# A two-layer attention trunk on one core: one tiling for the small matrix products, and the second layer's scale and shift computed inside the first layer's value products

## The chip, the cores and the metric

The kernel runs on one core of one Trainium2 chip, as one launch. The metric is device time in microseconds (us), from the start of the launch to its end. Before the change the median of three runs is 308.79 us (307.97 to 309.48).

A core has a matrix engine (TensorE; PE in the profile, with its weight loads listed apart as PEld), three engines that work on vectors (VectorE or DVE, ScalarE or ACT, GpSimd or POOL) and an engine that issues transfers (SyncE or SP). Each engine takes its own instructions strictly in the order in which they were written. SBUF is the on-chip memory, PSUM the memory that the matrix engine writes into.

## What is computed

The input is 256 tokens of width 1024. Two layers follow, each of this form:

```python
for i in range(DEPTH):                      # 2 layers
    shift, scale, gate = jnp.split(cond @ ada_w[i] + ada_b[i], 3, axis=-1)
    h = rms_norm(x, norm_g[i]) * (1 + scale[:, None, :]) + shift[:, None, :]
    y = nsa_mixer(h, ...) if i == 0 else moba_mixer(h, ...)
    x = x + gate[:, None, :] * y
```

`cond` is one row of 1024 numbers, `ada_w[i]` is 1024 x 3072. So scale and shift of a layer come from a product of one row with 2048 columns, and the gate from one with 1024 columns.

The first mixer is causal attention with 16 query heads and 4 key/value heads of width 64, in three branches whose results are added with a learned weight each: a windowed branch, a selected branch (with 256 tokens, all blocks are selected, so that it is causal attention with keys and values of its own), and a compressed branch. For the compressed branch, 15 overlapping blocks of 32 tokens are turned by a small two-layer network into one key and one value each. All is multiplied by `silu(z)` and goes through an output matrix:

```python
hid   = gelu(flat @ cmp_w1[i] + cmp_b1[i])          # blocks of 32 tokens x 64 -> 256
o     = g0 * softmax(q k_cmp) v_cmp + g1 * softmax(q k_sel) v_sel + g2 * softmax(q k_win) v_win
y     = (o * silu(z)) @ w_out
```

The second mixer is plain causal attention of the same shape with one branch. Everything is float32.

## The kernel before

**Precision.** The large products are made of three faster ones. A weight block of 128 x 1024 (`raw`) is rounded by ScalarE into `hi`, VectorE computes the rest `lo`, and the matrix engine adds hi x hi, hi x lo and lo x hi. Products whose operands stay plain float32 run as two matmul instructions each, so the profile counts two where the code has one call.

**Stages, in order of time.** The first 66 us or so load, scale and project the first layer's keys and values. Then come the compressing network (`cmp_steps`), the queries (`make_q`), the compressed keys and values, the gate blocks z (`z_blocks`), the first layer's attention (`pair_a(i)` for eight pairs of heads, i = 0 to 7), the output product (`out_products`), `next_h` for the second layer, its projections, its attention (`pair_b`, `values_b`) and its output product.

**Tiled products.** The matrix engine is an array of 128 x 128. A product that needs only some of its columns or rows can be placed on a part of it (`tile_position`), and several such parts work at the same time. The kernel before uses three ways of cutting:

- 128 rows x 32 columns, four parts: scale and shift (`ada_rows`, `ada_all`). The weights are the conditioning row in a 128 x 32 block (`condz`), and the data are 128 x 512 pieces of `ada_w`.
- 128 rows x 64 columns, two parts: the values (`values`, for both layers) and the compressing network (`cmp_steps`). For values, the two parts are the two heads of a pair.
- 32 rows x 128 columns, four parts: the compressed values. `Vbd` holds, for each pair j of a half (hf), 32 rows: 16 compressed blocks for each of two heads, in a block-diagonal form. `pcT` holds the transposed probabilities of eight heads in its 128 rows, so pair j needs rows 32j to 32j + 31. For two pairs at a time, this product opens the accumulators `ov[hf, j]`, to which `values` then adds.

**Side work.** `side` is a list of generators that run one step at a time where the program calls `beside()`: the four steps of the compressing network, then `ada_all` (the second layer's scale and shift, eight steps of two 512 KB loads and four products each, and an end with a copy, four transposes and three small VectorE operations into `AB`), then `ada_gate(0)` (a memset, eight steps of one 512 KB load and one VectorE accumulation into `gate`, and an end with two products and two copies). `beside()` is called once per step of the query product (four times), once for three of the z steps, and three times in each pair of the first six.

**Who decides the order.** The program does not run as it is written. `Plan` records every operation with what it reads and writes, and `issue` then orders the operations of each engine with a cost model: at each step the earliest possible operation of all engines is issued, ties being settled by level (FIRST_OF_ALL, URGENT, CHAIN, FILL) and then by number. A `plan.group()` is one unit that stays together. For the matrix engine the model adds `SWITCH` when the way of cutting changes, prefers tiled work while it is in a tiled state (`TILED`), and halves the clock after a stretch of 3.4 us with little work. `LATER_BY` moves single operations up or down among their equals by number, and `HOLD` gives single operations an earliest time. `Tag`s are sets of buffers: `raw` has 6, `ps` (PSUM) 6, `n_out` 2. SyncE issues all large loads in the planned order and waits where a buffer isn't free.

All instructions are written through one recording helper, so they all carry its line, L406, in the profile. They are told apart by the names of what they write and read: `ps<-raw,condz` is scale and shift of the second layer, `ps<-pT,VA` the values, `ps<-pcT,Vbd` the compressed values, `ps<-p,p` and `ps<-zT,p` the compressing network, `gate<-raw,condz,gate` the accumulation of a gate.

Of the kernel before, what the change touches and what calls it, by code (L numbers as in the profile page):

```python
# [56 lines left out]
    120: 16500, 167: 22100, 305: 52600, 312: 37600, 383: 32300, 385: 34800, 390: 48600, 395: 51100, 499: 79600,  # L57
    503: 79600, 951: 114700, 1239: 173400, 1371: 179400, 1543: 193600, 1558: 197000, 1625: 208400, 1715: 225000,
    1717: 227500, 1746: 205600, 2238: 273000,
# [13 lines left out]
class Plan:  # L73
# [179 lines left out]
    def issue(self, opening=()):  # L253
# [51 lines left out]
        while done < len(ops):  # L305
# [58 lines left out]
            if e == "T":  # L364
                tick = int(start // TICK)
                if op["mode"] != mode:
                    cost += SWITCH
                mode = op["mode"]
                cost = cost * (1 / 2.4 if tally.get(tick - 1, 0.0) >= 3060.0 else 1 / 1.2)
                tally[tick] = tally.get(tick, 0.0) + op["cost"]  # L370
                if (start + cost) // TICK > tick:
                    cost += PAUSE
# [61 lines left out]
def kernel(  # L434
# [133 lines left out]
    emask = const.tile([P, 2], F32, name="emask")  # L568
    V.tensor_reduce(emask, identF.rearrange("p (j e n) -> p e j n", e=2, n=16), axis=AX.XY, op=OP.add)
# [157 lines left out]
    def ada_all():  # L727

        acc = tile_of("ps", 512)
        for kk in range(8):  # L730
            w = [ada_piece(1, kk, c0, D)[:, 0] for c0 in (0, D)]
            with plan.at(FILL), plan.group():
                for s in range(2):
                    for h in range(2):
                        j = 2 * s + h
                        T.matmul(acc[32 * j:32 * j + 32], condz[:, kk], w[s][:, 512 * h:512 * h + 512],
                                 start=(kk == 0), stop=(kk == 7), tile_position=(0, 32 * j))
            if kk < 7:
                yield
# [214 lines left out]
    def values(o, parts, first):  # L954

        with nullcontext() if plan.open else plan.group():
            for n, (v, pT) in enumerate(parts):
                for e in range(2):
                    T.matmul(o[64 * e:64 * e + 64, 0:S], v[0], pT[e][:, 0:S], start=(first and n == 0), stop=False,
                             tile_position=(0, 64 * e))  # L960
                for e in range(2):
                    T.matmul(o[64 * e:64 * e + 64, P:S], v[1], pT[e][:, S:S + P], start=False,
                             stop=(n == len(parts) - 1), tile_position=(0, 64 * e))
# [248 lines left out]
    def cmp_steps(hid):  # L1212

        for kq in range(4):
            w1 = [[load(bass.AP(tensor=nsa_cmp_w1.tensor, offset=nsa_cmp_w1.offset + (kv * 2048 + kq * 512 + k * P) * 256,
                                ap=[[256, P], [P * 256, 2], [1, 256]]), W1_HOME[k // 2]) for kv in range(2)] for k in (0, 2)]
            with plan.at(FILL), plan.group():
                for k in range(4):
                    for kv in range(2):
                        T.matmul(hid[64 * kv:64 * kv + 64, 0:256],  # L1220
                                 FLAT[kv][kq // 2][:, 4 * (kq % 2) + k].rearrange("p g n -> p (g n)"), w1[k // 2][kv][:, k % 2, :],
                                 start=(kq == 0 and k == 0), stop=(kq == 3 and k == 3), tile_position=(0, 64 * kv))
# [4 lines left out]
    side += [cmp_steps(hid), ada_all(), ada_gate(0)]  # L1227
# [65 lines left out]
    Vbd = const.tile([P, 2, P], F32, name="Vbd")  # L1293
    for hf in range(2):
        for cc in range(2):
# [5 lines left out]
        V.tensor_mul(Vbd[:, hf].rearrange("p (e d) -> p e d", e=2),  # L1301
                     vb[:, None, hf * HD:(hf + 1) * HD].to_broadcast([P, 2, HD]),
                     emask[:, :, None].to_broadcast([P, 2, HD]))
# [10 lines left out]
    pcT, ov = {}, {}  # L1314

    def compressed(hf):
# [25 lines left out]
        A.copy(pcT[hf], t[:, 0:S])  # L1342

    def pair_a(i):
# [36 lines left out]
        if j_ % 2 == 0:  # L1381
            with plan.group():
                for j in range(j_, j_ + 2):
                    ov[hf, j] = tile_of("ps", 512)
                    T.matmul(ov[hf, j][:, 0:S], Vbd[32 * j:32 * j + 32, hf], pcT[hf][32 * j:32 * j + 32],
# [182 lines left out]
```

## Time and profile before

| | before |
|---|---|
| median of three runs | 308.79 us (307.97 to 309.48) |
| span of the profiled execution | 306.3 us |
| PE busy | 297.5 us, 97% of the span |
| VectorE busy | 248.7 us, 81% |
| ScalarE busy | 203.0 us, 66% |
| read from device memory | 64.36 MB |
| granted clock of the matrix engine, mean | 0.998 |

The page gives the span of the profiled execution, from its first to its last instruction, and no time of its own for that execution; the median lies 2.5 us above the span. Busy times of the matrix engine include the pipeline of each instruction, so that its work is better read from the distance of the starts of successive instructions. "Waited for" in the profile means the idle time just before an instruction and what ended it; "issue" is idle time that nothing in the profile explains.

### The profile page before, as it was taken

The numbers are of one execution on the slowest core, as the hardware profiler recorded it, in microseconds if no ns is written. First come the engines' busy times: TensorE is split into PE (matmuls) and PEld (weight loads), VectorE is DVE, ScalarE is ACT, GpSimd is POOL, SyncE is SP. The second block draws the span as 40 slices with busy tenths as digits, with TensorE's granted clock in tenths as the row PEclk, the third lists the DMA queues.
The fourth block names the chain that finished last, engine by engine and source line by source line (L and its number), as shares of the span: only waits on it lengthen the run. The fifth ranks groups of instructions, "written<-read, shape, count | busy, mean of one in ns | idle before, by whom it ended". The sixth has DMA issues, their size and how long they took to land.

```text
span 306.3 us, 6115 instructions
## 1 busy us (share of the span) xinstructions
PE 297.5 (97%) x2097; PEld 242.2 (79%) x2097; DVE 248.7 (81%) x736; ACT 203.0 (66%) x484; POOL 29.4 (10%) x100
## 2 busy tenths in 40 slices
PE   4999999999999999999999999999999999999995
PEld 4666777868878696878897788787788999878784
DVE  3674474678799988799999897797599999999664
ACT  4735244674937795679877985766566589999510
POOL 8128980000000000000000000000000000000000
PEclk9999999999999999999999999999999999999999
DMA  8999999699974294968558269036477780441002
GB/s 250 321 355 368 367 355 342 229 271 323 347 284 149 63 372 140 346 207 328 162 185 274 70 205 329 17 76 224 131 258 235 235 285 4 149 131 67 2 34 103
DMA packets 41099, 65.80 MB, mean 215 GB/s; under 512 B 4220, under 2 KB 20970, under 8 KB 41068
## 3 DMA queue, kind: packets, MB, share of 16 engines
q1 hardware_dynamic: 40708, 65.36, 65.0%
q8 instruction: 16, 0.26, 0.3%
q14 instruction: 15, 0.12, 0.1%
q10 hardware_dynamic: 168, 0.06, 0.1%
q0 software_dynamic: 192, 0.00, 0.0%
HBM read 64.36 MB, written 1.05 MB: 214 GB/s over the span
## 4 chain that ended last, share of the span: by engine, by line
PE 82%; DVE 6%; ACT 5%; DMA 4%; issue 2%; ACTq 0%; SPq 0%; DVEq 0%
PE ps L406 46%; PE acc L406 36%; DVE p L406 3%; ACT p L406 2%; DMA y<-in_ada_b_dram 2%; DMA early<-in_nsa_w_in_dram 1%; DMA raw<-in_nsa_w_out_dram 1%; DVE lo L406 1%; ACT pT L406 1%; ACT n_out L406 1%; DVE tiny L406 0%; ACT hi L406 0%; ACT HT L406 0%; ACT qg L406 0%; ACTq L406 0%
## 5 line engine op out<-in xcount | busy, mean ns | idle before, releaser
L406 ACT CAST hi<-raw 128x1024 fp32r<-128x1024 f32 (+1 forms) x48 | 49.2, 1027 | 17.1 <-PE acc L406 14.8
L406 DVE TENSOR_TENSOR lo<-raw,hi 128x1024 fp32r<-128x1024 f32 (+1 forms) x48 | 56.7, 1188 | 3.1 <-ACT hi L406 2.8
L406 ACT ACTIVATE p<-p,tiny 128x128 f32<-128x128 f32 (+1 forms) x96 | 43.2, 459 | 10.7 <-DVE tiny L406 10.6
L406 PE MATMUL acc<-hi,HT 128*128 128x512 f32 (+1 forms) x160 | 49.6, 383 | 0.0
L406 PE MATMUL acc<-HT,hi 128*128 128x256 f32 x192 | 39.1, 288 | 0.0
L406 PEld LDWEIGHTS acc<-hi,HT 128*128 128x128 f32 x160 | 28.8, 188 | 6.7 <-issue 1.2
L406 DVE CUSTOM_DVE_ANT_0 p<-ps,causal 128x128 f32<-128x128 f32 (+1 forms) x96 | 31.3, 356 | 1.5 <-PE ps L406 1.5
L406 PEld LDWEIGHTS acc<-HT,hi 128*128 128x128 f32 x192 | 30.5, 189 | 0.9 <-issue 0.7
L406 PE MATMUL acc<-lo,HT 128*128 128x512 f32 (+1 forms) x80 | 30.4, 384 | 0.4 <-DVE lo L406 0.4
L406 PE MATMUL ps<-hi,HT 128*128 128x512 f32 (+1 forms) x96 | 29.0, 367 | 0.0
L406 PE MATMUL ps<-KTA,qg 128*128 128x256 f32 (+2 forms) x192 | 27.3, 282 | 0.0
L406 PE MATMUL acc<-HT,lo 128*128 128x256 f32 x96 | 27.3, 286 | 0.0
L406 PEld LDWEIGHTS ps<-KTA,qg 128*128 128x128 f32 x192 | 24.2, 189 | 3.3 <-issue 1.2
L406 PE MATMUL ps<-hi,qg 128*128 128x256 f32 (+1 forms) x96 | 24.4, 324 | 0.0
L406 PE MATMUL acc<-hi,qg 128*128 128x512 f32 x64 | 23.3, 415 | 0.0
L406 ACT COPY pT<-ps 128x384 f32<-128x384 f32 x48 | 21.1, 492 | 2.3 <-PE ps L406 2.3
L406 DVE TENSOR_TENSOR lo<-early,hi 128x1024 fp32r<-128x1024 f32 (+2 forms) x17 | 17.4, 1041 | 5.4 <-ACT hi L406 5.0
L406 ACT CAST hi<-early 128x1024 fp32r<-128x1024 f32 (+2 forms) x17 | 14.8, 897 | 10.3 <-DMA early<-in_nsa_w_in_dram 8.5
L406 PE MATMUL ps<-identF,p 128*128 128x128 f32 x144 | 21.0, 275 | 0.2
L406 PEld LDWEIGHTS ps<-hi,HT 128*128 128x128 f32 x96 | 17.2, 188 | 4.6 <-issue 1.9
L406 DVE SCALAR_TENSOR_TENSOR gate<-raw,condz,gate 128x1024 f32<-128x1024 f32 x16 | 20.5, 1283 | 0.0
L406 PEld LDWEIGHTS ps<-identF,p 128*128 128x128 f32 x144 | 16.2, 140 | 3.8 <-DVE p L406 0.9
(218 smaller groups left out, 618.8 us busy)
## 6 DMA issues: line engine op xcount, KB each, us to landing
raw<-in_ada_w_dram SPq DMA_DIRECT2D x32, 512.0 KB, 5.7
raw<-in_moba_w_in_dram SPq DMA_DIRECT2D x20, 512.0 KB, 4.7
early<-in_ada_w_dram SPq DMA_DIRECT2D x12, 512.0 KB, 9.6
raw<-in_nsa_w_in_dram SPq DMA_DIRECT2D x12, 512.0 KB, 6.6
early<-in_nsa_w_in_dram SPq DMA_DIRECT2D x9, 512.0 KB, 9.2
raw<-in_nsa_w_out_dram SPq DMA_DIRECT2D x8, 512.0 KB, 4.6
raw<-in_moba_w_out_dram SPq DMA_DIRECT2D x8, 512.0 KB, 4.0
early<-in_nsa_w_in_dram SPq DMA_DIRECT2D x9, 256.0 KB, 6.0
```

The source lines that it names most:

```text
L406: r = getattr(self.engines[e], method)(*[self._real(a) for a in args], **{k: self._real(a) for k, a in kw.items()})
```

## The change

It has five parts.

1. **One tiling.** `values` and `cmp_steps` cut the array into four parts of 128 x 32 in place of two of 128 x 64: each call becomes two, with half of the weight columns each.
2. **Zero-padded compressed values.** `Vbd` becomes 128 x 2 x 4 x 128: for each pair it holds all 128 rows, with zeros outside the pair's 32 rows and outside the block diagonal. `emask` gets eight columns for it. The product takes all of `pcT`, in four parts of 128 x 32, and stands at the head of the pair's own values group. The accumulator is taken there, one for each pair. `Vbd` lives in a buffer of `n_out` now.
3. **Scale and shift of the second layer in the values groups.** `ada_all` leaves `side` and becomes `along`. Its first loads are recorded ahead of the first pair; step i's four products join the values group of pair i, and the loads of the next step follow. Its end comes with pair 7.
4. **Side work.** With `ada_all` gone, the gate's steps come sooner (the first in the fourth step of the query product, three in z), and each pair has one step.
5. **Plan.** The model keeps the full clock for every operation that starts after 20 us (`DEEP`), and `LATER_BY` and `HOLD` are another table, for the new numbers.

```diff
 LATER_BY = [
-    (109, 110, -64), (255, 255, 155), (307, 310, -51), (316, 317, -56), (330, 330, 298), (350, 350, 26),
...
+    (96, 96, 56), (161, 161, -76), (308, 308, -51), (309, 309, -14), (330, 330, 286), (345, 345, 357),
...
 HOLD = {
-    120: 16500, 167: 22100, 305: 52600, 312: 37600, 383: 32300, 385: 34800, 390: 48600, 395: 51100, 499: 79600,
...
+    93: 15600, 167: 22100, 235: 24800, 387: 44100, 390: 47900, 522: 63700, 781: 109200, 930: 121400, 1080: 117700,
...
-                cost = cost * (1 / 2.4 if tally.get(tick - 1, 0.0) >= 3060.0 else 1 / 1.2)
+                cost = cost * (1 / 2.4 if start > DEEP or tally.get(tick - 1, 0.0) >= 3060.0 else 1 / 1.2)
...
-    emask = const.tile([P, 2], F32, name="emask")
-    V.tensor_reduce(emask, identF.rearrange("p (j e n) -> p e j n", e=2, n=16), axis=AX.XY, op=OP.add)
+    emask = const.tile([P, 8], F32, name="emask")
+    V.tensor_reduce(emask, identF.rearrange("p (h n) -> p h n", n=16), axis=AX.X, op=OP.add)
...
             w = [ada_piece(1, kk, c0, D)[:, 0] for c0 in (0, D)]
-            with plan.at(FILL), plan.group():
-                for s in range(2):
-                    for h in range(2):
-                        j = 2 * s + h
-                        T.matmul(acc[32 * j:32 * j + 32], condz[:, kk], w[s][:, 512 * h:512 * h + 512],
-                                 start=(kk == 0), stop=(kk == 7), tile_position=(0, 32 * j))
-            if kk < 7:
-                yield
+            yield
+            for s in range(2):
+                for h in range(2):
+                    j = 2 * s + h
+                    T.matmul(acc[32 * j:32 * j + 32], condz[:, kk], w[s][:, 512 * h:512 * h + 512],
+                             start=(kk == 0), stop=(kk == 7), tile_position=(0, 32 * j))
+            yield
...
             for n, (v, pT) in enumerate(parts):
-                for e in range(2):
-                    T.matmul(o[64 * e:64 * e + 64, 0:S], v[0], pT[e][:, 0:S], start=(first and n == 0), stop=False,
-                             tile_position=(0, 64 * e))
-                for e in range(2):
-                    T.matmul(o[64 * e:64 * e + 64, P:S], v[1], pT[e][:, S:S + P], start=False,
-                             stop=(n == len(parts) - 1), tile_position=(0, 64 * e))
+                for j in range(4):
+                    T.matmul(o[32 * j:32 * j + 32, 0:S], v[0][:, j % 2 * 32:j % 2 * 32 + 32], pT[j // 2][:, 0:S],
+                             start=(first and n == 0), stop=False, tile_position=(0, 32 * j))
+                for j in range(4):
+                    T.matmul(o[32 * j:32 * j + 32, P:S], v[1][:, j % 2 * 32:j % 2 * 32 + 32], pT[j // 2][:, S:S + P],
+                             start=False, stop=(n == len(parts) - 1), tile_position=(0, 32 * j))
...
-                    for kv in range(2):
-                        T.matmul(hid[64 * kv:64 * kv + 64, 0:256],
-                                 FLAT[kv][kq // 2][:, 4 * (kq % 2) + k].rearrange("p g n -> p (g n)"), w1[k // 2][kv][:, k % 2, :],
-                                 start=(kq == 0 and k == 0), stop=(kq == 3 and k == 3), tile_position=(0, 64 * kv))
+                    for j in range(4):
+                        kv, half = divmod(j, 2)
+                        flat = FLAT[kv][kq // 2][:, 4 * (kq % 2) + k].rearrange("p g n -> p (g n)")
+                        T.matmul(hid[32 * j:32 * j + 32, 0:256], flat[:, 32 * half:32 * half + 32], w1[k // 2][kv][:, k % 2, :],
+                                 start=(kq == 0 and k == 0), stop=(kq == 3 and k == 3), tile_position=(0, 32 * j))
...
-    side += [cmp_steps(hid), ada_all(), ada_gate(0)]
+    side += [cmp_steps(hid), ada_gate(0)]
+    along = ada_all()
...
-    Vbd = const.tile([P, 2, P], F32, name="Vbd")
+    Vbd = tile_of("n_out", 2, 4, P)
...
-        V.tensor_mul(Vbd[:, hf].rearrange("p (e d) -> p e d", e=2),
-                     vb[:, None, hf * HD:(hf + 1) * HD].to_broadcast([P, 2, HD]),
-                     emask[:, :, None].to_broadcast([P, 2, HD]))
+        V.tensor_mul(Vbd[:, hf].rearrange("p j (e d) -> p (j e) d", e=2),
+                     vb[:, None, hf * HD:(hf + 1) * HD].to_broadcast([P, 8, HD]),
+                     emask[:, :, None].to_broadcast([P, 8, HD]))
...
+    next(along)
...
-        if j_ % 2 == 0:
-            with plan.group():
-                for j in range(j_, j_ + 2):
-                    ov[hf, j] = tile_of("ps", 512)
-                    T.matmul(ov[hf, j][:, 0:S], Vbd[32 * j:32 * j + 32, hf], pcT[hf][32 * j:32 * j + 32],
-                             start=True, stop=False, tile_position=(32 * j, 0))
-        o = ov[hf, j_]
+        o = tile_of("ps", 512)
         vs = slice(g * HD, (g + 1) * HD)
-        values(o, [([VA[:, m, 1 - r, vs] for m in range(2)], pT[r]) for r in (1, 0)], False)
+        with plan.group():
+            for j in range(4):
+                T.matmul(o[32 * j:32 * j + 32, 0:S], Vbd[:, hf, j_, 32 * j:32 * j + 32], pcT[hf], start=True, stop=False,
+                         tile_position=(0, 32 * j))
+            values(o, [([VA[:, m, 1 - r, vs] for m in range(2)], pT[r]) for r in (1, 0)], False)
+            next(along)
+        next(along, None)
         gated(i, o, zT[i])
...
-        beside(3 if i < 6 else 1)
+        beside()
```

More of the change, by code (lines that the diff above doesn't have):

```diff
@@ L56 @@
 HOLD = {
-    120: 16500, 167: 22100, 305: 52600, 312: 37600, 383: 32300, 385: 34800, 390: 48600, 395: 51100, 499: 79600,
-    503: 79600, 951: 114700, 1239: 173400, 1371: 179400, 1543: 193600, 1558: 197000, 1625: 208400, 1715: 225000,
-    1717: 227500, 1746: 205600, 2238: 273000,
[3 rows of a table added]
 }
@@ L1311 @@
     z_later = z_blocks(w_in, 3120, zT)
-    pcT, ov = {}, {}
+    pcT = {}
     def compressed(hf):
```

17 rows, old and new, of tables (HOLD, LATER_BY) are left out of this document.

## The prediction

> **What bounds the kernel now.** I read the page's engine shares first, then the chain that ended last, then the view by windows (busy time and count of each engine, clock, DMA share, GB/s) for the two stretches in which the edits act.
>
> ```profile
> span 306.3 us, 6115 instructions
> PE 297.5 (97%) x2097; PEld 242.2 (79%) x2097; DVE 248.7 (81%) x736; ACT 203.0 (66%) x484; POOL 29.4 (10%) x100
> ...
> PE 82%; DVE 6%; ACT 5%; DMA 4%; issue 2%; ACTq 0%; SPq 0%; DVEq 0%
> ```
>
> ```profile
> 66.00:118.00 52.00, 52.00 (x396) 42.41 (x397) 47.22 (x162) 36.10 (x82) 0.00 (x0) 1.00 0.74 253
> 118.00:188.00 70.00, 69.80 (x545) 56.28 (x546) 64.31 (x206) 54.97 (x158) 0.00 (x0) 1.00 0.65 221
> ```
>
> The matrix engine is busy for 97% of the span, at the full clock in both stretches, and 82% of the chain lies on it. So an edit brings its change in matrix work, plus what it takes from that engine's remaining waits. From 66 to 118 us (compressing network, queries, half of z) and from 118 to 188 us (the first layer's attention) it has next to no whole gap, while VectorE is busy for 91% and 92%. The waits left in the second stretch show at the weight loads (total us, times, longest):
>
> ```profile
> PEld ps L406 <- DVE tiny L406: 1.1, 3, 0.5
> PEld ps L406 <- DVE p L406: 0.8, 1, 0.8
> PEld ps L406 <- DVE gate L406: 0.8, 1, 0.8
> PEld ps L406 <- ACT pT L406: 0.3, 2, 0.2
> PEld ps L406 <- ACT pcT L406: 0.3, 1, 0.3
> PEld ps L406 <- ACT gate L406: 0.3, 1, 0.3
> ```
>
> VectorE and ScalarE stand behind 3.6 us of them. That is about what a better order could win here.
>
> **The change part by part: matrix work.** The matrix engine's timeline gives start, length, shape and count; the distance of two starts is the time that a run holds the engine.
>
> ```profile
> 16.06 1.08 PE L406 MATMUL ps<-early,condz 128*32 128x128 f32 x32
> 17.07 0.51 PE L406 MATMUL ps<-lo,HT 128*128 128x512 f32 x1
> ...
> 103.33 2.78 PE L406 MATMUL ps<-raw,condz 128*32 128x512 f32 x24
> 106.05 0.40 PE L406 MATMUL ps<-KTA,qg 128*128 128x32 f32 x2
> ...
> 117.87 1.11 PE L406 MATMUL ps<-pcT,Vbd 32*128 32x256 f32 x8
> 118.92 1.52 PE L406 MATMUL ps<-pT,VA 128*64 128x256 f32 x16
> 120.37 1.92 PE L406 MATMUL ps<-raw,condz 128*32 128x512 f32 x16
> 122.22 0.38 PE L406 MATMUL ps<-KTA,qg 128*128 128x256 f32 x1
> ...
> 123.39 0.39 PE L406 MATMUL acc<-HT,hi 128*128 128x256 f32 x2
> 123.61 0.28 PE L406 MATMUL acc<-HT,lo 128*128 128x256 f32 x1
> ...
> 131.48 0.39 PE L406 MATMUL acc<-HT,hi 128*128 128x256 f32 x2
> 131.80 1.52 PE L406 MATMUL ps<-pT,VA 128*64 128x256 f32 x16
> 133.25 1.06 PE L406 MATMUL ps<-raw,condz 128*32 128x512 f32 x8
> 134.25 0.44 PE L406 MATMUL ps<-identF,p 128*128 128x128 f32 x2
> ```
>
> *Rates.* Call four products on the four parts (eight instructions) a set. One set of 512 columns behind a values run takes 134.25 - 133.25 = 1.00 us, two take 122.22 - 120.37 = 1.85, three alone 106.05 - 103.33 = 2.72. So a set of 512 costs 0.86 us, and 0.13 us go to entering and leaving. Four sets of 128 columns take 17.07 - 16.06 = 1.01 us; less 0.13, one is 0.22 us. The time goes with the columns, so a set of 256 is 0.43 us. Untiled work in front of a tiled run stretches as well: the two products at 131.48 take 131.80 - 131.48 = 0.32 us, the same two at 123.39 take 0.22. That is 0.1 us more, and 0.23 us for going in and out together.
>
> *Values.* A run takes 120.37 - 118.92 = 1.45 us now, leaving included. In four parts it is two sets of 256 and two of 128: 2 x 0.43 + 2 x 0.22 = 1.30 us, and 1.43 with leaving. The products themselves gain nothing; the same holds for the compressing network and for the second layer's values, so those two together are worth 0.0 to -0.2 us.
>
> *Compressed values.* Now 118.92 - 117.87 = 1.05 us for pairs 0 to 3; pairs 4 to 7 take two runs of four instructions, of which this is the second:
>
> ```profile
> 149.06 0.70 PE L406 MATMUL ps<-pcT,Vbd 32*128 32x256 f32 x4
> 149.69 0.38 PE L406 MATMUL ps<-KTA,qg 128*128 128x256 f32 x1
> ```
>
> That is 0.63 us each, 2.3 us in all. After, each pair takes a set of 256: 8 x 0.43 = 3.4 us. The zero padding costs 1.1 us.
>
> *The sum of layer 1.* Before: eight values runs, 8 x 1.45 = 11.6; compressed values 2.3; scale and shift in runs of three, two and three times one set, 2.72 + 1.85 + 3 x 1.00 = 7.6; and eleven tiled runs that start out of untiled work (the first at 103.33, the last a values run of pair 7 at 179.64), 11 x 0.1 = 1.1. Together 22.6 us. After: eight runs of 0.43 + 1.30 + 0.86 + 0.23 = 2.82, together 22.6 us. **What the single tiling saves in changes, the padding spends: 0.0 us**, with bounds of -0.9 (no changes of cutting left but the eight, each at half price) and +0.8 (the padded sets as slow as the lone run, 0.63 - 0.43 = 0.2 more for each of four).
>
> At this place the Trainium skill has a rule against the change: the page TensorEngine Tiling (Array Packing), section Performance Considerations, gives each matmul an overhead of about 60 cycles and advises against drawing a tiling factor from a dimension that is small already. By that rule, the 16 added instructions in each of 12 values runs would add, as an estimate at the 2.4 GHz of the page TensorE: Matmul & The Clock Gate, section Part 1, 12 x 16 x 25 ns = 4.8 us. The row at 16.06 has 32 instructions of 128 columns in 1.01 us, 32 ns each, and sets of 512 columns take four times as long as sets of 128: nothing is left for an overhead, and the sum goes by 0.
>
> **VectorE, queues and waits.** From VectorE's groups of 118 to 188 us (count | busy us, mean ns), and from the list of what touches `Vbd` (ns, first and last start):
>
> ```profile
> L406 DVE SCALAR_TENSOR_TENSOR gate<-raw,condz,gate 128x1024 f32<-128x1024 f32 x8 | 10.3, 1283 | 0.0
> ```
>
> ```profile
> L406 DVE TENSOR_TENSOR Vbd<-ps,emask x2: 272/272/273, 93.8 to 98.1; 128x128 f32<-128x128 f32 x2
> ```
>
> All eight accumulations of the first gate lie in the attention stretch. By the program, four of them now come before pair 0: 4 x 1.28 = 5.1 us of VectorE leave a stretch where 64.3 of 70 us are taken, 84.6% from now on. I take half of the 3.6 us of waits as won: **-1.8 us**, between 0 (the waits are latencies, not load) and -3.6. Each of the two `Vbd` products grows from 128 to 512 columns: from 0.27 us to between 0.27 and 1.09 (four times), and I take 0.68, the middle, as the trace has no such shape: +0.8 us of VectorE for both, needed only at pair 0's values, some 20 us later; hidden. Both go to 66 to 118 us, where VectorE has 52.0 - 47.2 = 4.8 us free and gets 5.9: up to 1.1 us too much, and the matrix engine has 4 x 0.86 = 3.4 us less to do there, as four scale-and-shift sets move on. Cost 0 to 1.1; the work that hides it is the z products, which may stand anywhere, so I take 0. The end of `ada_all` (a copy, four transposes, three small operations) moves behind pair 7; `next_h` needs it only after the output product, which hides it. The rest (buffer of `n_out`, mask, clock rule) moves no busy engine; the clock rule only halves the model's clock, and the granted one is 1.00 in both stretches. The order table has no price in the trace: bounds are the 3.6 us once more and, for a loss, the rivals; I take 0.
>
> SP gets as many loads as before, but 14 of the 16 `ada_w` pieces now come one pair of loads per pair of heads, between those for z, gate and output matrix. Each values run waits for its two pieces. Behind it on the matrix engine stand the next pair's scores, and VectorE waits for those. The page's list of loads has the median time to landing, 5.7 us:
>
> ```profile
> raw<-in_ada_w_dram SPq DMA_DIRECT2D x32, 512.0 KB, 5.7
> ```
>
> From 85 to 188 us SP stood for a buffer behind `lo` eight times, 2.4 us on average:
>
> ```profile
> SPq L406 <- DVE lo L406: 19.1, 8, 8.7
> ```
>
> And the closest and the last values run of pairs 0 to 7:
>
> ```profile
> 137.24 1.52 PE L406 MATMUL ps<-pT,VA 128*64 128x256 f32 x16
> ...
> 179.64 1.52 PE L406 MATMUL ps<-pT,VA 128*64 128x256 f32 x16
> ```
>
> Runs are 137.24 - 131.80 = 5.4 us apart at the closest and (179.64 - 118.92) / 7 = 8.7 us on average. The 2.4 + 5.7 = 8.1 us that a piece needs fit the average. I take 0 and keep the close ones for a rival.
>
> **Sum:** 0.0 (tiling and padding) - 1.8 (waits) = -1.8 us, so a span of 304.5. The median is 308.79, 2.5 above the profiled span; 308.8 - 1.8 = **307.0 us**.
>
> **Rivals.** About 0.5% (1.5 us) is what a measurement of this kernel can tell from no change.
>
> *No change, 308.8 us.* The matrix work is the same and the waits are latencies of single chains, which a lighter VectorE doesn't shorten. For it speaks 97% busy; against it, that the longest waits end with VectorE.
>
> *Late pieces, 311.5 us.* The matrix engine stops inside a values run until its piece has landed. With the closest runs 5.4 us apart and 8.1 us needed, one such stop costs 2.7 us: 308.8 + 2.7. It decides where the two buffers come free less than 5.7 us ahead of the run. For it speaks that the pieces hold two of the six buffers from issue to run; against it, that the DMA share is only 0.65 here, so that an early issue finds a free queue.
>
> *VectorE overloaded before pair 0, 310.5 us.* The 1.1 us too much, and half of an accumulation (0.64 us) that stands in front of the chain's next operation and can't be broken off, start the attention 1.7 us later; it decides where the z products run out before. For it speaks that VectorE would be full from 66 to 118 us; against it, that it stands idle for 9.7 us of the 122 from 66 to 188 after the change as well, and that z products are left then.
>
> *Each matmul pays a floor, 314.9 us.* If each added instruction cost the shortest spacing seen, 32 ns: 12 x 16 x 32 ns = 6.1 us. Against it stands the row at 16.06, as above. It is the rule of the Trainium skill's page TensorEngine Tiling (Array Packing), section Performance Considerations.
>
> **How the numbers follow.** Forecast 0.42, no change 0.40, late pieces 0.11, VectorE 0.05, floor 0.02. The first gives faster 0.42, the second within 0.5% 0.40, the others slower 0.18. The range: below, all 3.6 us of waits are won, 305.2, less half of the tiling's bound, 304.8; above it reaches to 310.8, into the rivals of a loss. The forecast's own range is 305.2 to 307.3.
>
> **What would show it.** Right: values runs near 2.6 us from first to last start with `pcT,Vbd`, `pT,VA` and `raw,condz` in one stretch; four accumulations of `gate` before the first values run; VectorE near 85% from the first pair to the last, and the waits for `tiny`, `p` and `gate` halved. Wrong: a gap of the matrix engine inside a values run that ends with `raw<-in_ada_w_dram`; the first run later than 119 us with VectorE full before it; or sets of 128 columns well over 0.22 us.

## The result, and the profile after

The kernel after takes 310.6 us (median of 19 runs) against 308.85 us for the kernel before (19 runs on the same chips). The ratio is 1.0064, with a 95% interval of 1.0045 to 1.0082: it is **slower by some 2.0 us** (1.4 to 2.5). The forecast was 307.0 us, faster by 1.8. The time lies inside the range on record, and the direction was wrong. One of the 19 executions of after was disturbed and took 584 us: it counts in the median above (310.5 us without it), while ratios, and the medians of the runs below, leave such executions out. The profiled execution of after took 310.6 us with a span of 308.9, so it stands for the median. In every execution here that has both, the time lies 1.7 to 1.8 us above the span, so that the profiled execution of before, with a span of 306.3, took about 308.0 us, an estimate: the two profiles lie 2.6 us apart, the medians 1.75. The page of after begins:

```profile
span 308.9 us, 6709 instructions
PE 296.7 (96%) x2401; PEld 241.9 (78%) x2401; DVE 250.4 (81%) x736; ACT 202.4 (66%) x484; POOL 29.2 (9%) x100
...
PE 62%; DVE 16%; DMA 14%; issue 3%; ACT 2%; SPq 1%; ACTq 0%; DVEq 0%
```

There are 304 more matrix instructions, and the matrix engine is busy for 296.7 us where it was busy for 297.5. What changed is the chain that ended last: the matrix engine's share of it fell from 82% to 62%, VectorE's rose from 6% to 16% and that of transfers from 4% to 14%. The added time is waiting, not work. The shares themselves are not lost time: the chain of after goes back through two transfers of `early<-in_ada_w_dram` from 10.03 to 25.06 us, 15.0 us or 5% of the span, because of a single wait of 0.42 us:

```profile
25.10 1.07 PE L401 MATMUL ps<-early,condz 128*32 128x256 f32 x16 [0.42 <-DMA early<-in_ada_w_dram]
```

The view by windows tells where. It is the view shown in the prediction, first of before, then of after (window, its length, then busy us and instructions of PE, PEld, VectorE, ScalarE, GpSimd, the clock, the DMA share, GB/s):

```profile
13.00:66.00 53.00, 52.48 (x352) 38.64 (x351) 31.41 (x67) 28.02 (x53) 21.84 (x66) 1.00 1.01 327
66.00:85.00 19.00, 19.00 (x146) 14.59 (x146) 15.33 (x33) 12.41 (x22) 0.00 (x0) 1.00 0.98 334
85.00:118.00 33.00, 33.00 (x251) 27.83 (x252) 31.89 (x130) 23.68 (x61) 0.00 (x0) 1.00 0.61 206
```

```profile
13.00:66.00 53.00, 50.98 (x337) 36.89 (x338) 30.84 (x64) 25.84 (x47) 21.62 (x66) 1.00 1.00 324
66.00:85.00 19.00, 18.22 (x160) 15.12 (x159) 18.45 (x37) 14.71 (x27) 0.00 (x0) 1.00 0.94 307
85.00:118.00 33.00, 33.00 (x293) 29.22 (x292) 32.63 (x124) 21.08 (x54) 0.00 (x0) 1.00 0.48 163
118.00:188.00 70.00, 69.48 (x733) 54.23 (x733) 59.53 (x209) 55.26 (x165) 0.00 (x0) 1.00 0.68 226
```

Up to 85 us the matrix engine stands idle for 2.02 + 0.78 = 2.8 us, where it stood idle for 0.52 before: 2.3 us more, which is about what lies between the two profiles. VectorE takes 18.45 us of the 19 from 66 to 85 us instead of 15.33. Only one of the gate's accumulations is in that stretch, 1.28 us at 67.18; the other three that were moved ahead come at 86.61, 91.84 and 95.22 us. The rest of the 3.1 us is other work in another order, a second sum of squares (1.2 us) above all. In the attention stretch VectorE is lighter (59.53 of 70 us against 64.31, 85% as forecast), yet the matrix engine is no busier. The list of what the matrix engine waited for from 13 to 100 us has one entry before (total us, times, longest) and these in after:

```profile
PE acc L406 <- DVE lo L406: 0.4, 2, 0.2
```

```profile
PE ps L401 <- DMA p<-in_nsa_cmp_w_dram: 0.8, 1, 0.8
PE ps L401 <- DVE p L401: 0.6, 1, 0.6
PE acc L401 <- DVE HT L401: 0.6, 1, 0.6
PE ps L401 <- DMA early<-in_ada_w_dram: 0.4, 1, 0.4
PE acc L401 <- DVE lo L401: 0.3, 1, 0.3
PE ps L401 <- ACT VA L401: 0.2, 1, 0.2
```

All but the fifth are new, and they wait for different things: two loads, VectorE's copies into the compressing network's input (`p` at 63.45 us), a transposed input of the key and value projections (`HT`), a copy of values. The one for `HT` doesn't belong to the new order. It comes from one operation of VectorE, here with GpSimd's `memset` beside it, first in before, then in after:

```profile
42.55 0.51 DVE L406 TENSOR_SCALAR rot<-n_out,AB 128x256 f32<-128x256 f32 x1
43.59 0.95 POOL L406 MEMSET gate<- 128x1024 f32 x1
```

```profile
42.51 1.33 DVE L401 TENSOR_SCALAR rot<-n_out,AB 128x256 f32<-128x256 f32 x1
42.74 0.95 POOL L401 MEMSET gate<- 128x1024 f32 x1
```

In the 15 profiles that can be read (all but that of run 5), this operation takes 1.20 to 1.33 us in the seven in which the `memset` begins while it runs, and 0.41 to 0.52 us in the other eight; the wait for `HT` behind VectorE (0.6 to 0.7 us) is in those seven alone. Runs 1 and 11, with the order of before, are among the seven, and run 9, with the order of after, is not. So 0.6 of the 2.3 us is a matter of timing that befalls both kernels. That the `memset` lengthens the operation is read from this coincidence; no run moved it.

The largest is the second run of the compressing network, which begins 0.8 us after the engine ran dry. In the timeline (start, length, operation, wait before it) and in SyncE's own (first before, then after) one sees why:

```profile
76.48 0.30 PE L401 MATMUL acc<-hi,HT 128*128 128x304 f32 x1
77.56 1.07 PE L401 MATMUL ps<-p,p 128*32 128x256 f32 x16 [0.78 <-DMA p<-in_nsa_cmp_w_dram]
```

```profile
63.53 2.40 SPq L406 DMA_DIRECT2D raw<-in_nsa_w_in_dram  x2
67.06 0.88 SPq L406 DMA_DIRECT2D p<-in_nsa_cmp_w_dram  x2
```

```profile
64.93 6.06 SPq L401 DMA_DIRECT2D raw<-in_nsa_w_in_dram  x4
71.08 0.93 SPq L401 DMA_DIRECT2D p<-in_nsa_cmp_w_dram  x2
```

In the new order four loads of `raw` stand ahead of the compressing weights on SyncE's queue, where there were two. SyncE waits for a free buffer in front of them (from 50 to 80 us, 9.3 us behind `lo`, where it was 5.3), and the weights are issued 4.0 us later, 1.4 us of it because the first of the `raw` loads starts later.

The rows that the prediction named for the attention: the first pair's values run, and the waits at the weight loads from 118 to 190 us.

```profile
126.29 0.64 PE L401 MATMUL ps<-pcT,n_out 128*32 128x256 f32 x8
126.75 1.48 PE L401 MATMUL ps<-pT,VA 128*32 128x256 f32 x32
128.05 1.04 PE L401 MATMUL ps<-raw,condz 128*32 128x512 f32 x8
129.02 0.73 PE L401 MATMUL ps<-KTA,qg 128*128 128x256 f32 x4
```

```profile
PEld ps L401 <- DVE p L401: 1.7, 2, 0.8
PEld ps L401 <- DVE tiny L401: 0.8, 1, 0.8
PEld ps L401 <- DVE lo L401: 0.8, 1, 0.8
PEld ps L401 <- DVE g L401: 0.7, 1, 0.7
PEld acc L401 <- DVE g L401: 0.2, 1, 0.2
```

The run takes 129.02 - 126.29 = 2.73 us, and all eight look like this one: no run stops for a late piece of `ada_w`. The waits behind VectorE come to 4.2 us, where those behind VectorE and ScalarE were 3.6. They have other names but are not halved. Four accumulations of the gate come before the first values run, as forecast, and a fifth at 125.79 us, just ahead of it.

### The profile page after: what moved, and what is told of

Its sections match the earlier page's. It is cut to its first block, busy times and chain, and to the rows that moved or that the text cites. A ratio compares the mean times of both kernels' runs of the same rounds, so it can differ in the third digit from the quotient of the medians.

```text
span 308.9 us, 6709 instructions
## 1 busy us (share of the span) xinstructions
PE 296.7 (96%) x2401; PEld 241.9 (78%) x2401; DVE 250.4 (81%) x736; ACT 202.4 (66%) x484; POOL 29.2 (9%) x100
## 4 chain that ended last, share of the span: by engine, by line
PE 62%; DVE 16%; DMA 14%; issue 3%; ACT 2%; SPq 1%; ACTq 0%; DVEq 0%
PE ps L401 33%; PE acc L401 29%; DVE p L401 5%; DMA early<-in_ada_w_dram 5%; DVE lo L401 3%; DMA raw<-in_moba_w_in_dram 2%; DMA raw<-in_ada_w_dram 2%; DMA p<-in_nsa_cmp_w_dram 2%; DMA raw<-in_nsa_w_out_dram 2%; DVE gate L401 2%; DMA y<-in_ada_b_dram 2%; DVE n_out L401 1%; SPq L401 1%; ACT hi L401 1%; DVE n_parts L401 1%
## 5 line engine op out<-in xcount | busy, mean ns | idle before, releaser
L401 PE MATMUL acc<-HT,hi 128*128 128x256 f32 x192 | 38.0, 288 | 0.0
L401 DVE CUSTOM_DVE_ANT_0 p<-ps,causal 128x256 f32<-128x256 f32 (+1 forms) x96 | 30.2, 347 | 2.4 <-PE ps L401 2.3
L401 PE MATMUL ps<-hi,HT 128*128 128x512 f32 (+1 forms) x96 | 28.0, 361 | 0.0
L401 PE MATMUL ps<-KTA,qg 128*128 128x256 f32 (+2 forms) x192 | 26.1, 280 | 0.0
L401 PE MATMUL acc<-hi,qg 128*128 128x512 f32 x64 | 22.5, 402 | 0.0
L401 DVE TENSOR_TENSOR lo<-early,hi 128x1024 fp32r<-128x1024 f32 (+2 forms) x17 | 17.4, 1050 | 5.8 <-ACT hi L401 5.8
```

The costliest lines, as they stand in the source:

```text
L401: r = getattr(self.engines[e], method)(*[self._real(a) for a in args], **{k: self._real(a) for k, a in kw.items()})
```

## The experiments

Planning anew after any edit shuffles the whole program. So most kernels here have their engines' orders written out as lists (called **kept order** below), and an edit changes only the operations that it names. Code is shown in extracts, and the lists in short. A profile shows one execution; where that is 0.8 us or more off the median of its run, the text says so. Each run is compared with the kernel before on the same chip; ratios have 95% intervals, and "us" is the ratio's share of about 308.8.

**1. The tiling alone.** The kernel before in kept order; `values` and `cmp_steps` are cut as in the change, nothing else.

```diff
-                for e in range(2):
-                    T.matmul(o[64 * e:64 * e + 64, 0:S], v[0], pT[e][:, 0:S], ...
+                for j in range(4):
+                    T.matmul(o[32 * j:32 * j + 32, 0:S], v[0][:, j % 2 * 32:j % 2 * 32 + 32], pT[j // 2][:, 0:S], ...
```

> The kernel before with its own order of every engine written out and kept, and one edit: values and compressing network in four parts of 128 x 32. Both theories (the order costs the time; the padding and the pieces in the values runs cost it): the products take the same columns, 0 to -0.2 us, so 308.5 to 308.9 us. If each matmul paid a floor, 12 x 16 x 32 ns = +6.1 us, 315.

Measured: 309.16 us, ratio 1.0013 (0.9999 to 1.0026), +0.4 us, just not to be told from nothing. A floor for each matmul (+6.1 us) is excluded. The values got shorter, 17.0 us for all twelve against 17.4 (start to start). The second run of the compressing network got longer: from 73.26 to 75.84 it holds the engine for 2.58 us, where the same run took 74.19 - 72.32 = 1.87 in the kernel before.

```profile
73.26 1.56 PE L513 MATMUL ps<-p,p 128*32 128x256 f32 x14
74.45 0.39 PE L513 MATMUL ps<-zT,p 128*32 128x256 f32 x2
74.66 0.39 PE L513 MATMUL ps<-p,p 128*32 128x256 f32 x2
74.67 1.24 PE L513 MATMUL ps<-zT,p 128*32 128x256 f32 x14
75.84 0.41 PE L513 MATMUL acc<-lo,HT 128*128 128x304 f32 x1
```

Inside it stands a wait on the second step's weight load, seen at the matrix engine's weight loads from 66 to 85 us:

```profile
PEld ps L513 <- DMA p<-in_nsa_cmp_w_dram: 0.8, 2, 0.6
```

So the tiling is free within what can be measured, and the 0.7 us that this run got longer is a load that lands just then.

**2. The early order of before, in the kernel after**, for the operations of the first layer's keys and values, all of which stand ahead of the compressing network's first run (69.2 us in after, 66.0 in before); **3. its late order**, from the output product on; **4. the early order of after, in the kernel before**, for the same operations as in 2. In each, a part of the engines' lists is replaced by the other kernel's, in short:

```diff
-ORDER = {engine: order_of_after}
+ORDER = {engine: splice(order_of_before, order_of_after, at=...)}
```

> The changed kernel with its order written out, but the operations of the first layer's keys and values (all that are numbered below the first load of the compressing network, the same in both kernels) in the order in which the kernel before has them. Theory order: the changed kernel's loss arises before its first tiled run (69.2 us against 66.0), so about 2 us come back, 308.6 us. Theory structure (padding, pieces awaited in values runs): nothing comes back, 310.6 us.

> The changed kernel with its order written out, but everything from the first layer's output product on in the order of the kernel before. From there on the two kernels compute the same. Theory order, in its wide form (the new order loses some 0.9 us after 188 us too): 309.7 us. Theory that only the first 85 us lose: 310.6 us. Theory structure: 310.6 us.

> The kernel before with its order written out, but the operations up to the turning of the keys for the compressing network in the order of the changed kernel. Theory order: it loses what the changed kernel lost there, +2 us, 310.8 us. Theory structure: 308.8 us.

Measured: run 2 took 309.64 us, ratio 1.0039 (1.0022 to 1.0056), some 0.8 us less than after's 1.0064. Run 4 took 309.67 us, 1.0031 (1.0016 to 1.0047), 1.0 us more than before. The two swaps agree: the new early order costs 0.8 to 1.0 us, half of the 2 us expected; the first figure is a difference of two runs and good to about 0.8 us either way. In run 2 the waits for `p`, `HT` and `VA` are gone, and that on the compressing weights is longer:

```profile
PE ps L512 <- DMA p<-in_nsa_cmp_w_dram: 1.4, 1, 1.4
PE acc L512 <- DVE lo L512: 0.4, 2, 0.2
PE ps L512 <- DMA early<-in_ada_w_dram: 0.2, 1, 0.2
```

This execution took 308.32 us, 1.3 less than the median. Run 4's profile, 0.8 us faster than its median, shows none of the new waits of after, so where its 1.0 us goes was not seen.

Run 3 took 315.04 us, 1.0203 (1.018 to 1.0226): the old late order costs the kernel after another 4.3 us. It shows that the old late order is the worse one for this kernel, and no more than that: the old list was made for operations that are ready at other moments. Whether the new late order is as good in its place as the old one was in before isn't shown.

**5. and 6. The compressing weights earlier on SyncE's queue**, ahead of the last two of the four `raw` loads; in the kernel after (5), and together with the early order of before (6).

```diff
-        "S": [..., raw, raw, raw, raw, cmp_w, cmp_w, ...]
+        "S": [..., raw, raw, cmp_w, cmp_w, raw, raw, ...]
```

> The changed kernel with its order written out and one move on SP: the two loads of the compressing network's second step go ahead of the last two of the four weight loads that stand in front of them. Theory queue (SP stands behind full `raw` buffers, so the network's weights land late and the matrix engine stops 1.0 us at 76.5 us): 1 us comes back, 309.6 us. Theory that the stop only moves, because the weight loads are then late: 310.6 us or more.

> The changed kernel with the early order of the kernel before (309.64 us in the run without more) and the same move on SP. Theory queue: the stop of 1.4 us seen there goes, 308.2 us, at or under the kernel before. Theory that the stop only moves: 309.6 us.

Measured: run 5 took 310.94 us (five executions), 1.0079 (1.0051 to 1.0107), no gain over after. It has no profile that can be read. Run 6 took 309.87 us, 1.0028 (1.0011 to 1.0045), not to be told from run 2 (1.0039). The wait on the weights is gone from its trace, and waits behind `n_parts` stand there instead, 1.3 us. So the visible wait was the last of several conditions, as far as this one profile shows (its execution took 310.69 us, 0.8 above the median), and taking it away wins nothing that can be measured.

**7. The kernel after without the compressed products; 11. the kernel before without them.** Both in kept order.

```diff
-            for j in range(4):
-                T.matmul(o[32 * j:32 * j + 32, 0:S], Vbd[:, hf, j_, 32 * j:32 * j + 32], pcT[hf], start=True, stop=False,
-                         tile_position=(0, 32 * j))
-            values(o, [...], False)
+            values(o, [...], True)
```

> The changed kernel with its order written out, without the products of the compressed values (the compressed branch is left out of the sum). By the prediction's sum the attention stretch is bound by the matrix engine: 8 x 0.43 = 3.4 us less, 307.2 us. If VectorE bounds that stretch: 0 to -1 us, 310 us.

> The kernel before with its order written out, without the products of the compressed values (left out of the sum); their place in the order is dropped. If the attention stretch were bound by the matrix engine as the prediction took it: 2.3 us of products and 0.5 us of changes less, 306.0 us. If the waits for VectorE and ScalarE grow by what is taken away, as in the changed kernel without these products: 308.5 us.

Measured: run 7 took 310.62 us, 1.0059 (1.0036 to 1.0082). Eight sets of 0.43 us, 3.4 us of matrix work, are gone, and the time is that of after: the difference of the two ratios is 0.2 us, good to about 0.9 us either way, so that a gain above 1.1 us is excluded. The kernel before loses 2.8 us of work in the same way and wins 1.45 us: 307.64, 0.9953 (0.9937 to 0.9969). In run 7 the waits behind VectorE at the weight loads have grown:

```profile
PEld ps L512 <- DVE p L512: 3.7, 5, 1.9
...
PEld ps L512 <- DVE g L512: 1.0, 2, 0.7
PEld ps L512 <- DVE lo L512: 0.8, 1, 0.8
```

`p` went from 1.7 to 3.7 us, and all waits behind VectorE from 4.2 to 5.7, which is 1.5 of the 3.4 us; the profiled execution took 309.8 us, 0.8 less than the median, and where the rest went isn't shown. In the kernel after, taking matrix work out of the attention stretch no longer shortens the time by an amount that can be measured; in the kernel before about half of it comes back. A count of matrix instructions, on which the prediction's first step rested, doesn't decide the time there.

**8. Lighter accumulations in the attention, kernel before; 9. lighter accumulations before pair 0, kernel after; 10. those left out.** Four of the first gate's eight accumulations are cut from 1024 to 64 columns. The edit was reckoned at 4 x 1.2 = 4.8 us of VectorE; in the traces an accumulation went from 1.28 to 0.28 us, so it is 4.0 us. In the kernel after these four are the ones that were moved ahead; in run 10 their loads are gone too.

```diff
-                V.scalar_tensor_tensor(gate, w, condz[:, kk, 0:1], gate, op0=OP.mult, op1=OP.add)
+                n = 64 if l == 0 and kk < 4 else D
+                V.scalar_tensor_tensor(gate[:, :n], w[:, :n], condz[:, kk, 0:1], gate[:, :n], op0=OP.mult, op1=OP.add)
```

> The kernel before with its order written out, and four of the first gate's eight accumulations cut to 64 of their 1024 columns (the rest of these four is left out of the gate), so that VectorE has 4 x 1.2 = 4.8 us less in the attention stretch and all loads stay. Theory of the prediction: half of the 3.6 us of waits goes, 307.0 us. Rival: the waits are latencies, 308.8 us.

> The changed kernel with its order written out, and the first four of the first gate's eight accumulations cut to 64 of 1024 columns (the rest of these four is left out); the loads stay. Theory VectorE (the four accumulations fill VectorE ahead of the attention, 18.5 of 19 us busy from 66 to 85 us): 1 to 1.7 us less, 309.2 us. Theory buffers (what costs is that their pieces hold `raw` buffers and transfers): 310.6 us.

> The changed kernel with its order written out, without the loads and the accumulations of these four steps (left out of the gate). Theory VectorE: as with the narrow ones, 309.2 us. Theory buffers: 1.5 us or more less only here, 309.0 us, while the narrow ones stay at 310.6. If both stay at 310.6, the side work is not what costs.

Measured: run 8 took 308.3 us, 0.998 (0.9971 to 0.9989): the 4.0 us are worth 0.6 us in the attention of the kernel before, and its waits are hardly smaller (3.4 us behind VectorE and ScalarE, where it was 3.6):

```profile
PEld ps L513 <- DVE tiny L513: 1.9, 5, 0.8
...
PEld ps L513 <- DVE gate L513: 0.8, 1, 0.8
```

Run 9 took 309.63 us, 1.0027 (1.0007 to 1.0047), 1.1 us less than after, good to about 0.8 us either way. Its matrix engine has no gap from 66 to 118 us, and VectorE is down to 48.45 of 52 us; the profiled execution took 308.69 us, 0.9 less than the median:

```profile
66.00:118.00 52.00, 52.00 (x460) 44.97 (x459) 48.45 (x164) 36.55 (x81) 0.00 (x0) 1.00 0.64 210
```

Run 10 took 309.98 us, 1.0039 (1.002 to 1.0058): leaving out the loads and their buffers wins no more than the narrow form does, so it is VectorE's time and not the buffers. The move of four accumulations exchanged a place where 4.0 us of them cost 0.6 us for one where they cost 1.1. The difference of 0.5 is good to about 0.9 us either way; that the move didn't win 1.8 is certain, and that it lost 0.5 is likely and no more.

**12. The padded compressed values in the kernel before**, with the tiling, at the head of each values run as in the change; scale and shift stay where they were. Kept order.

```diff
-                    T.matmul(ov[hf, j][:, 0:S], Vbd[32 * j:32 * j + 32, hf], pcT[hf][32 * j:32 * j + 32],
-                             start=True, stop=False, tile_position=(32 * j, 0))
+            for j in range(4):
+                T.matmul(o[32 * j:32 * j + 32, 0:S], Vbd[:, hf, j_, 32 * j:32 * j + 32], pcT[hf], start=True, stop=False,
+                         tile_position=(0, 32 * j))
```

> The kernel before with its order written out, and parts 1 and 2 of the change: four parts of 128 x 32, and zero-padded compressed values at the head of each pair's own values run. Prediction's sum: padding +1.1 us, three stretches and changes fewer -0.7 us: 309.0 us with 0.4 us of the tiling alone 309.4. Theory that the attention stretch absorbs matrix work: 309.2 us, as the tiling alone. If waiting for the compressed probabilities is what costs: over 310 us.

Measured: 310.64 us, 1.0059 (1.0042 to 1.0076), 1.4 us more than the tiling alone (good to about 0.7 us either way), and 1.8 more than before. Both sums expected, 309.4 and 309.2, were too low. The time is the one named for waiting for the compressed probabilities, but the trace has no wait behind `pcT` from 85 to 190 us. What it has is work: tiled products take 35.9 us after 66 us, start to start, where run 1 has 34.7, and the matrix engine is busy for 299.1 us instead of 297.8. So all of the added work is felt, where half of the work taken away was felt in run 11: adding and taking away don't have one price in this order. Parts 1 and 2 alone cost nearly as much here as the whole change does in its own order. In the kernel after, where leaving the padded products out won nothing that can be measured (run 7), the padding itself was not taken out.

**13. and 14. Both kernels without an order table**, so that the planner's rule alone orders them. The two compare the structures, and with them the clock rule of part 5 (`DEEP`), which stays in, without either tuned order.

```diff
-LATER_BY = [(96, 96, 56), ...]
+LATER_BY = []
-HOLD = {93: 15600, ...}
+HOLD = {}
```

> The kernel after with both order tables (LATER_BY, HOLD) empty, so that the planner's rule alone orders it. Read against the next run, the kernel before with its tables empty as well. Theory (the loss lies in the order that the new table gives, above all before 100 us, not in the structure): without tables the two structures differ by under 1 us either way, or the new one is faster. Rival (the structure loses by itself: padding 1.4 us, accumulations ahead of pair 0 0.5 us): without tables the kernel after is 1 to 3 us slower than the kernel before without tables. Both are expected to lie 2 to 8 us above their tuned versions, since any foreign order has cost 1 to 4 us so far.

> The kernel before with both order tables empty: the partner of the run before. Theory (the order table loses): within 1 us of the kernel after without tables, or slower than it. Rival (the structure loses): 1 to 3 us faster than the kernel after without tables. 2 to 8 us above the kernel before with its tables, 311 to 317 us.

Measured: after without tables 312.49 us, 1.0107 (1.0089 to 1.0126); before without tables 311.85 us, 1.0096 (1.0079 to 1.0113). The difference is 0.3 us by the ratios (0.0011, within about 0.0025 or 0.8 us either way) and 0.6 by the medians. So, in the planner's own order, the **structure is worth 0.3 us of loss**, which can't be told from nothing. By the ratios the old table wins 0.0096 or 3.0 us over no table, the new one 1.0107 - 1.0064 = 0.0043 or 1.3 us: **the new table recovers 1.6 us less**, good to about 1 us either way. This is bookkeeping: what the structure doesn't cost without tables falls to the tables. Two readings remain that no run separates: the new table is the poorer one (33 entries for `LATER_BY`, where the old one has 64), or the new structure leaves less for any table to win. Run 12, where parts 1 and 2 cost 1.8 us in the old tuned order, speaks for the second in part. The page of run 13 gives the chain, and its timeline the second run of the compressing network:

```profile
PE 68%; DVE 18%; ACT 5%; issue 4%; DMA 3%; ACTq 0%; SPq 0%
```

```profile
75.01 1.07 PE L394 MATMUL ps<-p,p 128*32 128x256 f32 x16
75.90 1.05 PE L394 MATMUL ps<-zT,p 128*32 128x256 f32 x16
76.88 0.41 PE L394 MATMUL acc<-lo,HT 128*128 128x304 f32 x1
```

Without a table transfers have 3% of the chain, not 14%, and the run takes 76.88 - 75.01 = 1.87 us in the new tiling, just what the old tiling took. So the tiling doesn't bring the wait on the compressing weights with it; that wait comes with the order of after.

## Why the prediction was wrong, step by step

*Matrix work, 0.0 us: right.* Summed from start to start, all tiled work after 66 us takes 34.9 us against 34.6 (without 0.6 us of small products of the compressed keys, the same in both). A values run takes 2.73 us where 2.82 was summed, 0.1 of it for the work in front. Behind it, run 1 excludes the floor. The view that the padding costs 1.1 us and the single tiling pays for it holds as a sum of work for the whole change. What the step took for granted, that the time follows this sum, doesn't hold: work taken out is felt by half in the kernel before (run 11) and not measurably in the kernel after (run 7), and work put in is felt in full in the kernel before (run 12).

*"I take half of the 3.6 us of waits as won: -1.8 us": this step failed, and with it the sign.* VectorE's load in the attention was taken to cause those waits. Run 8 took 4.0 us of that load away without moving it and won 0.6 us, with 3.4 us of the waits left; the step named its other end itself ("the waits are latencies, not load"). And the load went to a place where it costs 1.1 us (run 9).

*VectorE in 66 to 118 us, "I take 0": failed.* The sum of loads was right (each product with the mask takes 0.67 us, 0.68 was taken; VectorE has 51.1 of 52 us, "full"). The z products do cover their own stretch: from 85 to 118 us the matrix engine has no gap. The gaps lie ahead of it, between 13 and 85 us, where single operands stop the engine in an order fixed beforehand; lighter accumulations win 1.1 us (run 9). The rival of an overloaded VectorE, given 0.05 and 310.5 us, has nearly the measured time, but that is luck: in it the z products run out before the attention, which they don't. Its sign, a first values run past 119 us, came true with 126.3 us, though that includes the reordering of queries and gates.

*"The order table has no price in the trace ... I take 0": failed, and by runs 13 and 14 it is the larger part.* Runs 13 and 14 put 1.6 us of the loss on the table as a remainder, and runs 2 and 4 find 0.8 to 1.0 us in the order of the first layer's keys and values. The bound for a loss was left to "the rivals", none of which was this one.

*Late pieces of scale and shift, 311.5 us: didn't happen.* No values run waits for `raw<-in_ada_w_dram`; one piece of it is late for VectorE, by 0.5 us, for the gate's accumulation at 135.60 us. The load that came late was another, the compressing weights behind two more `raw` loads on SyncE's queue, in a place where the step on SP ("as many loads as before") hadn't looked.

*What adds up and what doesn't.* 0.3 for the structure and 1.6 for the table make the 2.0 us measured (by the unrounded ratios), as they must. The other figures, +0.5 for the accumulations and 0.8 to 1.0 for the early order, are not further terms: they look at the same loss from other sides, and each is good to 0.5 to 0.9 us either way. The table's part holds whatever else its 33 entries and 21 holds do after the keys and values, which no run took apart. And since parts 1 and 2 cost 1.8 us in the old order but the whole structure 0.3 without tables, a price of a part holds only in the order in which it was measured. What the loss would be with a table tuned as long for the new structure stays open.

## What to carry to other kernels

Where an order was tuned for one program, an edit that renumbers the operations needs another table: run both versions without their tables as well (here the tables were worth 3.0 and 1.3 us) before asking what the edit itself is worth. A wait that a busy engine ends is not necessarily won by making that engine less busy (here 0.6 us for 4.0); ask whether the single operation that ends it starts earlier. And when work is moved to where its engine has "enough free time in the sum", look at the operand that stands next in line there.

## What the runs showed of the chip that was not expected

- Removing 3.4 us of matrix products from a stretch where the matrix engine is busy for 99% (69.48 of 70 us) changed nothing that can be measured (run 7). Busy time near 100% doesn't show that an engine sets the end. The shares of the chain (62% against 82%) pointed the right way, but a single short wait moves them by 5% of the span.
- The kernel after has the wider spread. 18 of its 19 executions lie between 308.8 and 312.5 us, the 19 of before between 307.7 and 309.7; 14% of its chain are transfers, against 4%. The five of run 13, with 3%, lie between 311.7 and 312.7. That the transfers cause the spread was not tested.
- An operation of VectorE (128 x 256, `rot<-n_out,AB`) takes 1.20 to 1.33 us when GpSimd's `memset` of 0.95 us begins while it runs, and 0.41 to 0.52 us otherwise, in 15 of 15 profiles. It ends about when the `memset` does (43.84 and 43.69 us in after).
- With products on several parts of the array, starts need not follow the written order. In the lines of run 1, two instructions of `ps<-zT,p` begin at 74.45 us, ahead of the last two of `ps<-p,p` at 74.66, which stand before them in the program. The statement above that each engine takes its instructions strictly in written order is too strong there.
- The four-part tiling costs no more than the two-part one: 32 instructions of a values run in the second layer take 1.44 us, and 16 with twice the weight columns 1.45.
